# Second attention of a two-layer encoder: score products with packed rows, and a set of four 32-row rotary products between two units' full ones

## The chip, the cores and the metric

One NeuronCore of a Trainium2 chip runs the whole program in one launch. The time is the device time of one execution in microseconds; the smaller the better. Matrix products run on PE (TensorE), whose weight loads the profile calls PEld; DVE is VectorE, ACT is ScalarE, POOL is GpSimd, and SP is the queue that issues most DMAs.

## The reference

Two layers over x of shape (1, 1024, 1024) in float32. Layer A is a dilated window attention; layer B, which the change touches, is a latent attention with 16 heads:

```python
def mixer_mla(u, w_in, q_norm, w_uq, kv_norm, w_ukv, w_out):
    cq, ckv, k_rope, gate = jnp.split(u @ w_in, [256, 256 + 128, 256 + 128 + 32], axis=-1)
    q = (rmsnorm(cq, q_norm) @ w_uq).reshape(B, S, 16, 64 + 32)
    q_nope, q_rope = q[..., :64], q[..., 64:]
    kv = (rmsnorm(ckv, kv_norm) @ w_ukv).reshape(B, S, 16, 64 + 64)
    k_nope, v = kv[..., :64], kv[..., 64:]
    q_rope = rope(q_rope, cos[:, None], sin[:, None])
    k_rope = rope(k_rope, cos, sin)              # one rotary key for all heads
    # per block of 128 queries, per head
    s = (q_nope . k_nope + q_rope . k_rope) * 96 ** -0.5
    o = softmax(s) @ v
    return (o * silu(gate)) @ w_out
```

(The two sums of products are written here with a dot.) Each layer ends with `x <- LayerNorm(alpha * x + gate_c * mixer(u))`.

## The kernel before

Every float32 product is made of three products in PE's faster float32 form: an operand is split into a high part (the rounded value) and a low part (the rest), and high x high, high x low and low x high are added in PSUM (`mm3`; its three lines L92 to L94 appear under those numbers in the profile wherever it is called).

The program runs layer A's attention, its gate and output, then layer B's latents (`layer_b_in`), its gate (`gate`), the second attention (`layer_b_attention`) and the output (`layer_b_out`). The order of PE and SP is the order in which the code is written (`FIXED`); on ACT, DVE and POOL a scheduler chooses the order when the program is built. `weave` interleaves generators of PE work by the costs that they yield.

The second attention works in 128 units of one head (`u // 8`) and one block of 128 queries (`u % 8`). Two heads are a pair of heads `p`; two units, below, a pair of units. For a unit:

- `front(u)`: scores of 128 queries by 1024 keys into an `s` tile of two PSUM banks (two such tiles): for each half of the keys `mm3` with 128 rows, of which 64 hold the head's own part and 64 the rotary part of two heads (32 of the 64 rows of the key are zeros for the wrong head);
- `soft(u)`: DVE takes the row maximum `mb`; `expo(u)`: ACT makes the exponential `pr` and its sum `den`;
- `middle(u)`: PE transposes `pr` in eight 128x128 pieces into two banks `t` (four banks serve `t`, `o` and the projections `m`); ACT casts the high part `pth`, DVE subtracts for the low part `ptl`;
- `back(w)`: for a pair of units, sixteen products of 256 columns with V into `o`; ACT copies out two pieces `osum`, POOL adds them and multiplies the gate `gT`. `spread` sends the reciprocal sums through DRAM to `rden`, with which POOL multiplies later (`normalise`).

Between units run the projections for the next heads: `b_turn` (rotary rows of q for four heads: PE, four DVE products with cos and sin, POOL sums), `b_qk` (q and k of two heads) and `b_v`. For each head the key tiles `kb` (three in turn) got the shared rotary key rows by a POOL copy, `b_rope_rows`. `kb`, `pr`, `osum`, `ab`, `rope` come from a pool `H` of 14 tiles; `q`, `pth`, `ptl`, `vq`, `gT`, the latents `lat` from a pool `G` of 33.

Of the kernel before, what the change touches and what calls it, by code (L numbers as in the profile page):

```python
# [23 lines left out]
P = 128  # L24
# [45 lines left out]
class Trunk:  # L70
# [944 lines left out]
    def layer_b_in(self):  # L1015
# [11 lines left out]
        self.kb = [[self.ht(F32R, "kb") for _ in range(2)] for _ in range(2)]  # L1027

# [22 lines left out]
        nc.gpsimd.memset(latn, 0.0)  # L1051
        ln = [latn[:, 0:512], latn[:, 512:1024]]

        def latents(i):
# [8 lines left out]
            tmp = self.M.tile([P, 64], F32, tag="krt", bufs=2, name=self.nm("krt"))  # L1063
# [19 lines left out]
        def latents_t(i):  # L1083
# [5 lines left out]
            for e, (h, l) in enumerate(self.kb):  # L1089
                dst.append((h[64:128, c : c + P], l[64:128, c : c + P], slice(64 - 64 * e, 128 - 64 * e), 3))  # L1090
            for h, l, rows, j in dst:
                src = pt[rows, j * P : j * P + P]
                nc.scalar.copy(h, src)
                nc.vector.tensor_tensor(l, src, f32(h), op=ALU.subtract)

# [18 lines left out]
        self.wu, self.wv, self.q, self.gT = {}, {}, {}, []  # L1114
# [16 lines left out]
        for b in range(8):  # L1131
# [14 lines left out]
            if b == 0:  # L1146
                self.kb.append([self.ht(F32R, "kb") for _ in range(2)])
                self.b_rope_rows(2)
# [10 lines left out]
        weave((chain(gate(6, 1, self.mbank), gate(7, 1, self.mbank)), 10368.0), (chain(self.b_turn(0), self.b_qk(0)), 9000.0))  # L1159
# [78 lines left out]
    def b_turn(self, p):  # L1238


        nc = self.nc
        r1 = self.ht(F32, "rope")
        self.rope = {p: [], p + 1: [r1[64:128, 0:512], r1[64:128, 512:1024]]}
        for hf in range(2):
# [10 lines left out]
            r0 = ab[64:128, 512:1024]  # L1255
            for dst, row, op in (
                (r1[64:96, sl], 32, ALU.subtract),
                (r1[96:128, sl], 96, ALU.add),
                (r0[32:64], 64, ALU.add),
                (r0[0:32], 0, ALU.subtract),  # L1260
            ):
                nc.gpsimd.tensor_tensor(dst, ab[row : row + 32, 0:512], ab[row : row + 32, 512:1024], op=op)
            self.rope[p].append(r0)

    def b_qk(self, p):

# [4 lines left out]
        qe = [self.gt(F32R, "q") for _ in range(2)]  # L1271
        qo = [self.gt(F32R, "q") for _ in range(2)]
        self.q[2 * p], self.q[2 * p + 1] = qe, qo
        ke, ko = self.kb[(2 * p) % 3], self.kb[(2 * p + 1) % 3]
        rr = self.rope.pop(p)

        def put(dst, sl, src):
            nc.scalar.copy(dst[0][0:64, sl], src)
            nc.vector.tensor_tensor(dst[1][0:64, sl], src, f32(dst[0][0:64, sl]), op=ALU.subtract)

        def rope(hf, part):
            sl = slice(hf * 512, hf * 512 + 512)
            for q in (qe, qo):
                if part == 0:
                    nc.scalar.activation(q[0][64:128, sl], rr[hf], AF.Copy)
                else:
                    nc.gpsimd.tensor_tensor(q[1][64:128, sl], rr[hf], f32(q[0][64:128, sl]), op=ALU.subtract)

        if p:
            self.b_rope_rows(2 * p)  # L1290
            self.b_rope_rows(2 * p + 1)
# [24 lines left out]
    def layer_b_attention(self):  # L1316
# [4 lines left out]
        def front(u):  # L1321
# [7 lines left out]
            if t == 7:  # L1329
                self.q.pop(hd)  # L1330
# [349 lines left out]
```

## Time and profile before

| | |
|---|---|
| time, median of 3 runs | 1356.77 us (1356.26 to 1359.17) |
| profiled execution | 1356.85 us, its span 1355.1 us |
| PE busy | 1328.6 us, 98% of the span |
| PEld, DVE, ACT, POOL busy | 1143.5, 855.9, 799.1, 565.3 us |
| granted clock of PE | 0.994 mean |
| second attention, first to last score product | 776.2 to 1244.7 us |

A row of a timeline has the start in the span, the duration, engine, source line, operation, out<-in, sizes and count; in brackets the time that the engine was idle before it and what ended that. A product's row shows how long it is in the array and its pipeline, not what the next one waits.

### The profile page before, as it was taken

The page shows a single profiled execution, that of the slowest core. Times are in us where ns is not written, and L with a number is a line of the kernel's source. Part 1 is how long each engine was busy: PE and PEld are TensorE (multiplying, and loading weights), DVE is VectorE, ACT ScalarE, POOL GpSimd, SP SyncE. Part 2 cuts the span into 40 slices and gives each one's busy share as a digit, 9 for nine tenths or more (in the row PEclk, how much of TensorE's full clock was granted, in tenths as well). Part 3 has the DMA queues.
Part 4 walks back from the last instruction along what each step waited for, and adds up shares of the span by engine and source line. Part 5 has one row for each costly group of instructions (what it writes and reads, how often), then busy time and mean ns, then how long its engine had stood idle before and what let it go on. Part 6 is the DMA issues. An engine that isn't in the chain of part 4 may idle for free.

```text
span 1355.1 us, 20458 instructions
## 1 busy us (share of the span) xinstructions
PE 1328.6 (98%) x7435; PEld 1143.5 (84%) x7435; DVE 855.9 (63%) x1480; ACT 799.1 (59%) x1631; POOL 565.3 (42%) x552
## 2 busy tenths in 40 slices
PE   9999999999999999999999999999999999999997
PEld 7888888888888888888988888898889889898776
DVE  7645445445544345376733378878787788777887
ACT  4665556544444423165632397889698878887411
POOL 0333123213231477425533444734654473444861
PEclk8999999999999999999999999999999999999999
DMA  9423211113244374371163011111121111113322
GB/s 369 146 35 64 33 58 54 49 27 126 96 132 132 92 179 160 124 252 47 50 182 115 2 33 34 24 38 25 32 52 28 30 25 28 25 55 124 110 93 93
DMA packets 45117, 114.30 MB, mean 84 GB/s; under 512 B 6893, under 2 KB 13342, under 8 KB 45017
## 3 DMA queue, kind: packets, MB, share of 16 engines
q1 hardware_dynamic: 40204, 100.41, 24.0%
q0 software_dynamic: 4192, 12.27, 3.7%
q8 instruction: 59, 0.97, 0.3%
q14 instruction: 42, 0.34, 0.1%
q10 hardware_dynamic: 620, 0.31, 0.1%
HBM read 96.43 MB, written 8.67 MB: 78 GB/s over the span
## 4 chain that ended last, share of the span: by engine, by line
PE 78%; DVE 7%; ACT 7%; DMA 3%; issue 3%; SPq 0%; ACTq 0%; DVEq 0%
PE pj L92 8%; PE pj L94 8%; PE pj L93 8%; PE o L1396 6%; PE t L1376 5%; PE po L92 4%; PE po L93 4%; PE po L94 4%; PE s L92 3%; PE s L94 3%; PE s L93 3%; PE pg L92 2%; PE pg L93 2%; PE pg L94 2%; PE ip L272 2%
## 5 line engine op out<-in xcount | busy, mean ns | idle before, releaser
L92 PE MATMUL pj<-uh,wh 128*128 128x512 f32 x528 | 217.2, 411 | 0.7 <-ACT wh L104 0.7
L94 PE MATMUL pj<-uh,wl 128*128 128x512 f32 x528 | 207.0, 392 | 0.0
L93 PE MATMUL pj<-ul,wh 128*128 128x512 f32 x528 | 206.8, 392 | 0.0
L1336 DVE TENSOR_REDUCE mb<-s 128x1 f32<-128x1024 f32 x128 | 155.8, 1217 | 48.7 <-PE s L94 47.9
L1380 DVE TENSOR_TENSOR ptl<-t,pth 128x512 fp32r<-128x512 f32 x256 | 165.3, 681 | 5.2 <-ACT pth L1379 3.0
L1379 ACT CAST pth<-t 128x512 fp32r<-128x512 f32 x256 | 139.5, 590 | 37.4 <-PE t L1376 34.0
L1344 ACT ACTIVATE pr<-s,mb 128x1024 f32<-128x1024 f32 x128 | 144.2, 1126 | 15.4 <-DVE mb L1336 14.7
L105 POOL TENSOR_TENSOR wl<-wraw,wh 128x1024 fp32r<-128x1024 f32 x42 | 106.3, 2536 | 102.4 <-ACT wh L104 75.4
L1376 PEld LDWEIGHTS t<-ident,pr 128*128 128x128 f32 x1024 | 119.3, 141 | 19.1 <-DVE ptl L1380 2.8
L1376 PE MATMUL t<-ident,pr 128*128 128x128 f32 x1024 | 133.1, 273 | 2.1 <-DVE ptl L1380 2.1
L1396 PE MATMUL o<-pth,vq 128*128 128x256 f32 x512 | 130.4, 292 | 1.1 <-DVE ptl L1380 1.1
L1396 PE MATMUL o<-ptl,vq 128*128 128x256 f32 x512 | 125.6, 283 | 0.8 <-DVE ptl L1380 0.5
L564 ACT ACTIVATE sb<-sb,stat 128x256 f32<-128x256 f32 (+1 forms) x144 | 67.0, 466 | 94.8 <-DVE stat L558 94.7
L94 PEld LDWEIGHTS pj<-uh,wl 128*128 128x128 f32 x528 | 99.1, 188 | 22.2
L1407 POOL TENSOR_TENSOR osum<-osum 64x256 f32<-64x256 f32 x64 | 47.9, 748 | 163.7 <-ACT osum L1406 162.6
L92 PEld LDWEIGHTS pj<-uh,wh 128*128 128x128 f32 x528 | 99.7, 189 | 15.1 <-ACT wh L104 1.1
L93 PEld LDWEIGHTS pj<-ul,wh 128*128 128x128 f32 x528 | 99.8, 189 | 14.0
L92 PE MATMUL s<-kb,q 128*128 128x512 f32 x256 | 105.8, 413 | 0.1
L94 PE MATMUL s<-kb,q 128*128 128x512 f32 x256 | 100.4, 392 | 0.0
L93 PE MATMUL s<-kb,q 128*128 128x512 f32 x256 | 100.4, 392 | 0.0
L1396 PEld LDWEIGHTS o<-ptl,vq 128*128 128x128 f32 x512 | 97.8, 191 | 1.7 <-DVE ptl L1380 1.7
L1396 PEld LDWEIGHTS o<-pth,vq 128*128 128x128 f32 x512 | 97.6, 191 | 1.8 <-DVE ptl L1380 1.7
(289 smaller groups left out, 3128.2 us busy)
## 6 DMA issues: line engine op xcount, KB each, us to landing
wraw<-wa SPq DMA_DIRECT2D x36, 512.0 KB
ada<-ada_row SPq DMA_DIRECT2D x64, 256.0 KB
wraw<-wo_a SPq DMA_DIRECT2D x18, 512.0 KB
ada<-ada_ss SPq DMA_DIRECT2D x16, 512.0 KB
kb<-kb POOLq DMA_DIRECT2D x30, 256.0 KB, 4.5
f<-f_d SPq DMA_DIRECT2D x18, 256.0 KB
xr<-x SPq DMA_DIRECT2D x8, 512.0 KB
xn_d<-z POOLq DMA_DIRECT2D x8, 512.0 KB, 4.5
```

What stands on the lines that cost most here:

```text
L92: mm(out, wh, xh, start=start, stop=False)
L93: mm(out, wh, xl, start=False, stop=False)
L94: mm(out, wl, xh, start=False, stop=stop)
L105: (lo_engine or self.nc.gpsimd).tensor_tensor(l[:, :width], raw[:, :width], f32(h[:, :width]), op=ALU.subtract)
L564: nc.scalar.activation(sb[:, a * w : a * w + w], sb[:, a * w : a * w + w], AF.Exp, bias=stat[:, 0, hh, t : t + 1], scale=-1.0, accum_out=s ...
L1336: nc.vector.tensor_reduce(m[:, 0:1], s, axis=AX.X, op=ALU.max, negate=True)
L1344: nc.scalar.activation(pr, s, AF.Exp, bias=m[:, 0:1], accum_out=dens[u // 8][:, u % 8 : u % 8 + 1])
L1376: nc.tensor.transpose(pt[:, c * P : c * P + P], pr[:, kt * P : kt * P + P], self.ident)
L1379: nc.scalar.copy(h, src)
L1380: nc.vector.tensor_tensor(l, src, f32(h), op=ALU.subtract)
L1396: nc.tensor.matmul(po[:, 0:256], v, pts[j][x][:, c * 256 : c * 256 + 256], start=n == 0, stop=n == 15)
L1407: nc.gpsimd.tensor_tensor(w3[mine, 0:256], w3[mine, 256:512], w3[mine, 0:256], op=ALU.add)
```

## The change

The score product is laid out anew. For a head there are now two key tiles and two query tiles of 128 rows, and a shared key tile `kr`:

- `k[0]` holds the high part of the head's 64 key rows twice, `qa` the high and the low part of the query: one product gives high x high and low x high;
- `k[1]` holds the low part of the 64 rows, 32 rows of the low part of the rotary key and 32 of its high part, `qb` the query's high part, the rotary query's high part and its low part;
- what is left, rotary high x rotary high, has 32 rows. `kr` holds the high rotary key in four groups of 32 rows (groups 0 and 2 the first 512 keys, 1 and 3 the others), `q3` the rotary query's high part likewise (groups 0 and 1 for the even block, 2 and 3 for the odd). The four products of a pair of units each take one group of rows of the array (`tile_position=(32 * g, 0)`) and one PSUM bank.

`front` now does a pair of units: four full products, the set of four, four full products. The loop steps by pairs, and the second unit's exponential is issued ahead of `back`. The rotary rows of q go through a DRAM tile `rope_d`, from which `qb` and `q3` are loaded; rows that stand twice are copied by a DMA on SP (for the first pair of heads by a second ACT cast). POOL's per-head copies of key rows go. `b_turn(0)` runs in one weave with the gate's next to last product, `b_qk(0)` with the last.

```diff
-            for c in (400, 448):
-                nc.vector.tensor_tensor(t[:, c : c + 16], tmp[:, 0:16], tmp[:, 32:48], op=ALU.subtract)
-                nc.vector.tensor_tensor(t[:, c + 32 : c + 48], tmp[:, 16:32], tmp[:, 48:64], op=ALU.add)
+            rot = t[:, 384:512].rearrange("p (g a c) -> p g a c", g=4, a=2)
...
+            for rows in ((slice(0, P),) if i < 4 else (slice(32, 64), slice(96, 128))):
+                nc.scalar.copy(self.kr[rows, sl], pt[rows, 3 * P : 4 * P])
...
-        weave((chain(gate(6, 1, self.mbank), gate(7, 1, self.mbank)), 10368.0), (chain(self.b_turn(0), self.b_qk(0)), 9000.0))
+        weave((gate(6, 1, self.mbank), 5184.0), (self.b_turn(0), 2600.0))
+        weave((gate(7, 1, self.mbank), 5184.0), (self.b_qk(0), 3900.0))
...
-    def b_rope_rows(self, hd):
-        for src, dst in zip(self.kb[(hd - 2) % 3], self.kb[hd % 3]):
-            self.nc.gpsimd.dma_start(dst[64:128, :], src[64:128, :])
+    def b_rope_rows(self):
+        dma, first = self.nc.gpsimd.dma_start, self.kb[0][1]
+        for j in range(2):
+            dma(first[96:128, j * 512 : j * 512 + 512], self.kr[32 * j : 32 * j + 32, :])
+        for n in (1, 2):
+            dma(self.kb[n][1][64:128, :], first[64:128, :])
...
+            engine = nc.gpsimd if p else nc.vector
+            for rows, op in ((slice(0, 64), ALU.subtract), (slice(64, 128), ALU.add)):
+                engine.tensor_tensor(ab[rows, 0:512], ab[rows, 0:512], ab[rows, 512:1024], op=op)
+            yield 0.0
+            hl = self.ht(F32R, "rope")
+            nc.scalar.activation(hl[:, 0:512], ab[:, 0:512], AF.Copy)
+            engine.tensor_tensor(hl[:, 512:1024], ab[:, 0:512], f32(hl[:, 0:512]), op=ALU.subtract)
+            for a in range(2):
+                for x in range(2):
+                    nc.sync.dma_start(rd[:, x, a, :, sl], f32(hl[64 * a : 64 * a + 64, x * 512 : x * 512 + 512]))
...
+            nc.sync.dma_start(f32(qb[64:128, :]), rows.rearrange("x a c t -> (x a c) t"))
+            q3 = third[:, e * 512 : e * 512 + 512]
+            for g in range(4):
+                src = rows[0].rearrange("a c (i z t) -> (a c) i z t", z=2, t=P)[:, :, g // 2, :]
+                nc.sync.dma_start(f32(q3[32 * g : 32 * g + 32, :]).rearrange("p (i t) -> p i t", t=P), src)
...
+        def both(dst, twin, sl, src, rows):
+            nc.scalar.copy(dst[0:64, sl], src)
+            if p:
+                nc.sync.dma_start(f32(twin[rows, sl]), f32(dst[0:64, sl]))
+            else:
+                nc.scalar.copy(twin[rows, sl], src)
...
+            def full(a):
+                ts = slice((t + a) * P, (t + a) * P + P)
+                for n, (q, kk) in enumerate(((qa, k[0]), (qb, k[1]))):
+                    for j in range(2):
+                        ks = slice(j * 512, j * 512 + 512)
+                        mm(s[a][:, ks], q[:, ts], kk[:, ks], start=n == a == 0, stop=n == a == 1)
+                st[u + a] = s[a]
+            full(0)
+            for g in range(4):
+                rows = slice(32 * g, 32 * g + 32)
+                ks = slice((g % 2) * 512, (g % 2) * 512 + 512)
+                mm(
+                    s[g // 2][:, ks], q3[rows, (t // 2) * P : (t // 2) * P + P], self.kr[rows, :],
+                    start=g >= 2, stop=g < 2, tile_position=(32 * g, 0),
+                )
+            full(1)
...
+        for u0 in range(0, nu + 4, 2):
+            if u0 < nu:
+                front(u0)
...
+                soft(u0)
+                soft(u0 + 1)
+                expo(u0)
+            for u in (u0, u0 + 1):
...
+                if 0 <= u - 2 < nu:
+                    middle(u - 2)
+                    next(vprep, None)
+                if u == u0 and u < nu:
+                    expo(u + 1)
+                if u == u0 and u >= 4:
...
+                    back((u - 4) // 2)
```

On PE, unit 82 before stood like this: six full products of 128 rows into its score tile, then the transposes of an earlier unit's exponential.

```order
L92 MATMUL s_1738_10422<-kb_830_5410,q_1653_10014 128x512
L93 MATMUL s_1738_10422<-kb_831_5411,q_1653_10014 128x512
L94 MATMUL s_1738_10422<-kb_830_5410,q_1654_10015 128x512
L92 MATMUL s_1738_10422<-kb_830_5410,q_1653_10014 128x512
L93 MATMUL s_1738_10422<-kb_831_5411,q_1653_10014 128x512
L94 MATMUL s_1738_10422<-kb_830_5410,q_1654_10015 128x512
L1376 MATMUL t_1744_10435<-ident_71,pr_1725_10363 128x128 x4
L1376 MATMUL t_1745_10442<-ident_71,pr_1725_10363 128x128 x4
```

On PE, units 82 and 83 now (`s_1747` and `s_1748` are their score tiles; L1357 is the 32-row set):

```order
L1350 MATMUL s_1747_10472<-kb_830_5410,q_1665_10069 128x512 x2
L1350 MATMUL s_1747_10472<-kb_831_5411,q_1666_10070 128x512 x2
L1357 MATMUL s_1747_10472<-kr_5412,q3_1664_10068 128x512 x2
L1357 MATMUL s_1748_10473<-kr_5412,q3_1664_10068 128x512 x2
L1350 MATMUL s_1748_10473<-kb_830_5410,q_1665_10069 128x512 x2
L1350 MATMUL s_1748_10473<-kb_831_5411,q_1666_10070 128x512 x2
L1408 MATMUL t_1756_10496<-ident_71,pr_1730_10404 128x128 x4
L1408 MATMUL t_1757_10503<-ident_71,pr_1730_10404 128x128 x4
```

Two units' scores, which were twelve full products in two places, are eight full ones with the set of four between them, in one place.

On ACT, the same units before: the exponentials (`pr`) with the casts of transposed tiles (`pth`) and the copies of `o` (`osum`) between them.

```order
L1344 ACTIVATE pr_1746_10449,den_1724_10362<-s_1738_10422,mb_1739_10429 128x1024
L1357 COPY rden_1748_10469<-o_1747_10451 4x128
L1405 COPY osum_1749_10473<-o_1747_10451 64x256
L1406 COPY osum_1749_10473<-o_1747_10451 64x256
L1379 CAST pth_1740_10431<-t_1755_10500 128x4x128
L1379 CAST pth_1742_10433<-t_1756_10507 128x4x128
L1344 ACTIVATE pr_1757_10514,den_1724_10362<-s_1752_10486,mb_1754_10498 128x1024
```

On ACT, these units now:

```order
L1376 ACTIVATE pr_1751_10490,den_1729_10403<-s_1747_10472,mb_1749_10486 128x1024
L1411 CAST pth_1752_10492<-t_1756_10496 128x4x128
L1376 ACTIVATE pr_1758_10510,den_1729_10403<-s_1748_10473,mb_1750_10488 128x1024
L1411 CAST pth_1754_10494<-t_1757_10503 128x4x128
L1389 COPY rden_1760_10531<-o_1759_10513 4x128
L1437 COPY osum_1761_10535<-o_1759_10513 64x256
L1438 COPY osum_1761_10535<-o_1759_10513 64x256
```

The second exponential moved ahead of the copies of `o`, with one cast between the two exponentials.

On ACT at the start of the attention before (`pg_960` is the gate's last product, `m` the projections that become q and k, `ab` the rotary rows, `s_963` the first score tile):

```order
L1278 CAST q_956_6643<-m_961_6682 64x512
L1285 ACTIVATE q_954_6641<-ab_953_6632 64x512
L1285 ACTIVATE q_956_6643<-ab_953_6632 64x512
L1128 ACTIVATE gT_946_6565<-pg_960_6672 128x512
L1221 CAST vq_964_6735<-m_968_6739 128x4x2x64
L1344 ACT_TABLE_LOAD
L1344 ACTIVATE pr_971_6749,den_970_6748<-s_963_6728,mb_969_6746 128x1024
```

On ACT at the same place now (`pg_955` is the gate's last product, `s_965` the first score tile, `q_957` and `q_958` are `qa` and `qb` of the first head):

```order
L1135 ACTIVATE gT_946_6539<-pg_955_6635 128x512
L1302 CAST q_957_6640<-m_961_6654 64x512
L1306 CAST q_958_6641<-m_961_6654 64x512
L1302 CAST q_957_6640<-m_963_6689 64x512
L1306 CAST q_958_6641<-m_963_6689 64x512
L1302 CAST q_959_6647<-m_961_6654 64x512
L1306 CAST q_960_6648<-m_961_6654 64x512
L1302 CAST q_959_6647<-m_963_6689 64x512
L1306 CAST q_960_6648<-m_963_6689 64x512
L1376 ACT_TABLE_LOAD
L1376 ACTIVATE pr_975_6753,den_974_6752<-s_965_6723,mb_972_6748 128x1024
```

The casts that make q of the first two heads moved from ahead of the gate's last activation to behind it.

More of the change, by code (lines that the diff above doesn't have):

```diff
@@ L1295, in b_qk @@
             yield 1300.0
-            put(qe, sl, ps[0:64, :])
-            put(qo, sl, ps[64:128, :])
+            for e, (qa, qb, k) in enumerate(heads):
+                src = ps[64 * e : 64 * e + 64, :]
+                both(qa, qb, sl, src, slice(0, 64))
+                nc.vector.tensor_tensor(qa[64:128, sl], src, f32(qa[0:64, sl]), op=ALU.subtract)
             yield 0.0
-            rope(hf, 0)
             ps = self.mbank()
```

151 lines of the change are left out of this document (63 added, 88 removed).

## The prediction, as put on record before the run

> **What bounds the kernel now.** I read the page's shares first, then the busy times by stretch, then TensorE's timeline over some pairs of units of the second attention, and last ACT's and DVE's timelines there.
>
> ```profile
> span 1355.1 us, 20458 instructions
> PE 1328.6 (98%) x7435; PEld 1143.5 (84%) x7435; DVE 855.9 (63%) x1480; ACT 799.1 (59%) x1631; POOL 565.3 (42%) x552
> ...
> 1020.00:1060.00 40.00, 39.50 (x265) 35.44 (x264) 30.54 (x42) 34.52 (x71) 17.37 (x20) 1.00 0.10 24
> 1060.00:1100.00 40.00, 39.13 (x262) 34.65 (x261) 33.49 (x47) 29.89 (x60) 23.12 (x24) 1.00 0.13 26
> ```
>
> In a stretch the columns are length, then busy time of PE, PEld, DVE, ACT and POOL, granted clock, DMA share. PE is busy 98% at clock 1.00, so only PE time that is taken out shortens the attention; ACT (34.5 of 40) and DVE (33.5 of 40) come next.
>
> ```profile
> L92 PE MATMUL s<-kb,q x256: 389/395/504, 776.2 to 1244.3; 128*128 128x512 f32 x128
> ...
> 1002.99 0.40 PE L92 MATMUL s<-kb,q 128*128 128x512 f32 x1
> 1003.22 0.40 PE L93 MATMUL s<-kb,q 128*128 128x512 f32 x1
> ...
> 1004.15 0.40 PE L94 MATMUL s<-kb,q 128*128 128x512 f32 x1
> 1004.38 1.03 PE L1376 MATMUL t<-ident,pr 128*128 128x128 f32 x8
> 1005.17 0.47 PE L92 MATMUL s<-kb,q 128*128 128x512 f32 x1
> 1005.49 0.39 PE L93 MATMUL s<-kb,q 128*128 128x512 f32 x1
> ...
> 1006.64 1.04 PE L1376 MATMUL t<-ident,pr 128*128 128x128 f32 x8
> 1007.43 0.36 PE L1396 MATMUL o<-pth,vq 128*128 128x256 f32 x1
> 1007.63 0.28 PE L1396 MATMUL o<-ptl,vq 128*128 128x256 f32 x1
> ...
> 1009.42 0.27 PE L1399 MATMUL o<-ident,den 128*4 128x128 f32 x1
> 1009.45 0.48 PE L92 MATMUL s<-kb,q 128*128 128x512 f32 x1
> ```
>
> The mean duration of a product (0.39 us) is not its price: they overlap, and the next starts 0.23 us later (six from 1002.99 to 4.38: 1.39/6 = 0.2317). Eight transposes take 0.79 us (1004.38 to 5.17), 0.099 each, every one with a weight load of its own. After transposes the first product costs 0.32 instead of 0.23 (1005.17 to 5.49): 0.09 us for a weight load that nothing covers. The sixteen products with V take 1.99. One pair: 12 x 0.2317 + 0.09 + 2 x 0.79 + 1.99 = 6.44 us, and the trace has 1002.99 to 1009.45 = 6.46, with no gap. With the projections between them the 64 pairs take from 776.2 to 1244.7, 7.3 us each.
>
> **The change, part by part.**
>
> *Removed and added on PE.* A pair had 12 full products of scores (3 kinds x 256 = 768 in all) and gets 8, plus four 32-row ones that lie in four row groups of the array and write four banks. That removes 4 x 0.2317 = 0.927 us a pair and adds the set, which no row of this trace shows. Its lower end is one full product, 0.23 (all four run at once). Its upper end is four in a row and an uncovered load on either side, as at a transpose: 0.93 + 2 x 0.09 = 1.11. A gain beyond the lower end is excluded, since 512 columns must still be streamed. Between them I go by the weight loads: each of the four has its own, and the nearest rows, the transposes, take one every 0.099. The product ahead of the set covers two (0.23/0.099), two are left: the last of the four starts 0.198 after the first and streams 0.23, then the return to the full array costs one uncovered load. 0.198 + 0.232 + 0.09 = 0.52. So 0.927 - 0.52 = 0.41 a pair, x 64 = **26 us**.
>
> *Second exponential ahead of the products with V, and both units in one step.* Now PE runs full products, set, full products, 8 transposes, 16 products with V, 8 transposes. Does the set's second half wait for the score bank of the unit before? Rows for the pitches of ACT and DVE:
>
> ```profile
> 1001.70 0.59 ACT L1379 CAST pth<-t 128x512 fp32r<-128x512 f32 x1
> 1002.18 1.12 ACT L1344 ACTIVATE pr<-s,mb 128x1024 f32<-128x1024 f32 x1
> 1003.19 0.20 ACT L1344 ACTIVATION_READ_ACCUMULATOR pr<-s,mb 128x1 f32 x1
> 1003.28 0.59 ACT L1379 CAST pth<-t 128x512 fp32r<-128x512 f32 x1
> 1003.89 0.37 ACT L1405 COPY osum<-o 64x256 f32<-64x256 f32 x1
> ...
> 1011.12 1.23 DVE L1336 TENSOR_REDUCE mb<-s 128x1 f32<-128x1024 f32 x1 [1.79 <-PE s L94]
> 1012.26 1.28 DVE L1380 TENSOR_TENSOR ptl<-t,pth 128x512 fp32r<-128x512 f32 x2
> 1013.46 1.22 DVE L1336 TENSOR_REDUCE mb<-s 128x1 f32<-128x1024 f32 x1
> ```
>
> Start to start: exponential 1.10, cast 0.48, maximum 1.14, two subtractions 1.20. From the pair's start F: first unit's scores at F+1.6, its maximum to 2.8, exponential 2.9 to 4.0, two casts to 5.0, second exponential 5.0 to 6.1. The next pair starts at F+6.0 and needs that bank at its set, F+7.0: 0.9 us to spare. The transposes use four banks in turn; the tightest reuse is that of the pair's last four, which take the bank of its first four: wanted at F+5.6, read by DVE up to F+5.25, 0.35 us to spare. ACT needs 2 x 1.10 + 4 x 0.48 + 2 x 0.37 = 4.9 of 6.0 us a pair, DVE 2 x 1.14 + 2 x 1.20 = 4.7. Hidden, while these margins hold; if they go, the bank is what is late next.
>
> *Preparation of queries and keys.* Before, ACT and POOL wrote the rotary rows of each head:
>
> ```profile
> L1278 ACT CAST q<-m 64x512 fp32r<-64x512 f32 x24 | 14.0, 582 | 4.6 <-DVE q L1279 4.5
> L1285 ACT ACTIVATE q<-ab 64x512 fp32r<-64x512 f32 x12 | 6.9, 620 | 0.1
> L1285 ACT ACTIVATE q<-rope 64x512 fp32r<-64x512 f32 x12 | 6.9, 620 | 0.1
> ...
> 1010.01 0.24 SPq L1358 DMA_DIRECT2D den_d<-rden  x1
> 1011.27 0.45 SPq L1359 DMA_DIRECT2D rden<-den_d  x1
> ```
>
> Of these, four ACT casts per pair of heads (4 x 0.62) go, and one 128x512 cast per half and two pairs of heads comes; POOL's subtractions and its copies of key rows go. SP gets 18 transfers per pair of heads and 8 more per two of them: 22 x 0.24 to 0.45 = 5 to 10 us of issuing in eight pairs (54 us). A write and the read that waits for it lie 1.26 us apart (1010.01 to 1011.27). The heads' rows are ready over one pair, some 7 us, ahead of use, so these hops are hidden. What queues behind a waiting SP transfer are the denominators' two; their reader is POOL, half idle, and PE waits for neither. Priced at nothing. In the three stretches with a rotation on POOL, the exponentials stand behind a cast that waits for it: I add 1 us in all.
>
> *The start of the attention* is not hidden:
>
> ```profile
> 774.53 0.58 ACT L1278 CAST q<-m 64x512 fp32r<-64x512 f32 x1
> 776.58 1.15 ACT L1285 ACTIVATE q<-ab 64x512 fp32r<-64x512 f32 x2 [1.46 <-POOL ab L1262]
> 777.75 0.60 ACT L1128 ACTIVATE gT<-pg 128x512 f32<-128x512 f32 x1
> ...
> 775.99 0.69 DVE L1279 TENSOR_TENSOR q<-m,q 64x512 fp32r<-64x512 f32 x1
> ...
> 776.02 0.39 PE L94 MATMUL pg<-u1h,wgl 128*128 128x512 f32 x1
> 776.24 0.39 PE L92 MATMUL s<-kb,q 128*128 128x512 f32 x1
> 779.12 1.28 ACT L1344 ACT_TABLE_LOAD   x1
> ```
>
> Before, the casts of q stood ahead of the last gate's activation; now all eight stand behind it (the order of ACT, above). The gate's last product ends at 776.41; then activation 0.60, cast 0.58, DVE's subtraction 0.69: the first score product at 778.3 instead of 776.24, 2.1 us. Seven casts (3.4) and the table load (1.28) then hold the first exponential, so that the second and third pair's sets wait some 0.6 us each: 3.3 us, less the 0.5 us (39.5 of 40) that PE already loses there: **+3 us**. The rest (latents, output projection) keeps its PE rows under a busy PE: nothing.
>
> **Sum.** -26 + 3 + 1 = -22. The profiled execution took 1356.85 (span 1355.1), 0.1 above the median 1356.77. I predict 1356.8 - 22 = **1334 us**.
>
> **Against the Trainium skill.** After transposes the trace's return to full products costs 0.09 us, and I charge the same once for the set. The Trainium skill, "TensorEngine Tiling (Array Packing)", section Tiling Modes, states that a change of the tiling mode drains TensorE; no run here shows it yet. It is the third rival below. The same skill's "TensorE: Matmul & The Clock Gate", Part 3, gives 3.07x for four 32-row products of 512 columns; an estimate by it is 0.93/3.07 = 0.30 for the set and, with 0.09, about 1322 us. That speaks for the first rival.
>
> **Rivals.**
> 1. *All four at once.* The loads of the set run ahead of all four: 0.232 + 0.09 = 0.32, 0.61 a pair, -39 + 4: **1322 us**. For it: weight loads do run under products in this trace (PEld 84% beside PE 98%). Against: nowhere here are more than one known to be ahead. Chance 0.25.
> 2. *Slower: the row groups run one after another.* Set 0.93, loads 0.18: 1.11 against 0.927 removed, +0.18 x 64 = +12, +4 of the start: **1373 us**. It decides from a set of 0.86 us on (0.927 - 4/64). For it: every product in this trace starts only after the one ahead has streamed. Against: none here lies in a row group of its own. Chance 0.15.
> 3. *A drain on both sides of the set.* A product's row ends 0.39 after its start, 0.16 after the next one's; paid twice, instead of the 0.09: 0.43 + 0.32 = 0.75, 0.18 a pair, -11 + 4: **1350 us**. Chance 0.13.
> 4. *The banks of the transposes.* If the 0.35 us of margin goes and each pair loses 0.3, the gain shrinks by 19: **1353 us**. For it: ACT and DVE at 84 to 86% of the stretch, and their stretch gets 6% shorter. Chance 0.07.
>
> **Numbers.** The forecast's own case (set between 0.4 and 0.65, 1326 to 1342) has 0.40. A measurement here tells about 0.2%, 2.7 us, from no change. Faster: 0.40 + 0.25 + 0.13 + most of 0.07 = 0.82; slower 0.15; the same 0.03. The range runs from a set at its lower end with no uncovered load (0.695 x 64 = 44, less 4: 1317) to rival 4 with some spread: **1316 to 1356**, which leaves the slower rival out.
>
> **What would show it.** After: 512 full score products and 256 of 32 rows; the step from the set's first start to the next full product reads 0.32 (rival 1), 0.5 (forecast), 0.75 (3) or 1.1 (2). A pair without projections takes 6.05 us. PE idles 2 us ahead of the first score product, behind DVE's q. Wrong would be: PE waiting within each pair for DVE's ptl (rival 4) or PE's share falling under 95%.

## The result and the profile after

The changed kernel takes 1377.05 us (median of 4 runs, 1376.94 to 1377.24), the kernel before 1357.97 beside it: **19 us slower**, ratio 1.0138 (95% interval 1.0119 to 1.0158). The forecast was 1334. The page of the profiled execution, then the groups of the score products, and the stretches that the prediction quoted for the kernel before (columns: length, busy time of PE, PEld, DVE, ACT, POOL, granted clock, DMA share):

```profile
span 1375.2 us, 20612 instructions
PE 1321.1 (96%) x7435; PEld 1104.8 (80%) x7435; DVE 871.9 (63%) x1462; ACT 788.0 (57%) x1611; POOL 489.1 (36%) x479
```

```profile
L1350 PE MATMUL s<-kb,q x512: 387/396/796, 785.1 to 1261.1; 128*128 128x512 f32 x171
L1357 PE MATMUL s<-kr,q x256: 489/491/792, 790.7 to 1259.8; 32*128 32x512 f32 x128
```

```profile
1020.00:1060.00 40.00, 37.90 (x273) 32.19 (x272) 31.12 (x42) 32.04 (x65) 11.93 (x14) 1.00 0.10 29
1060.00:1100.00 40.00, 37.99 (x252) 30.77 (x251) 31.00 (x42) 32.87 (x65) 14.23 (x16) 1.00 0.27 68
```

PE did become 7.5 us less busy, but it now stands idle 2.1 us in each 40 (0.5 and 0.9 before), and the attention begins at 785 in place of 776. ACT and DVE are about as busy as before.

To place the loss I cut both executions at the first product of the latents and at the exponentials of pairs of units 0, 4 and 60. These rows are from the timelines of PE and ACT, first of the kernel before, then of the changed one:

```profile
637.10 0.43 PE L92 MATMUL plat<-wlh,u1h 128*128 128x416 f32 x1
780.42 1.12 ACT L1344 ACTIVATE pr<-s,mb 128x1024 f32<-128x1024 f32 x1
802.69 1.12 ACT L1344 ACTIVATE pr<-s,mb 128x1024 f32<-128x1024 f32 x1
1221.28 1.13 ACT L1344 ACTIVATE pr<-s,mb 128x1024 f32<-128x1024 f32 x1
```

```profile
640.70 0.43 PE L92 MATMUL plat<-wlh,u1h 128*128 128x416 f32 x1
792.83 1.12 ACT L1376 ACTIVATE pr<-s,mb 128x1024 f32<-128x1024 f32 x1 [4.21 <-DVE mb L1368]
817.07 1.12 ACT L1376 ACTIVATE pr<-s,mb 128x1024 f32<-128x1024 f32 x1 [0.45 <-DVE mb L1368]
1240.68 1.11 ACT L1376 ACTIVATE pr<-s,mb 128x1024 f32<-128x1024 f32 x1
```

| stretch, us | before | after | difference | forecast | step of two alone |
|---|---|---|---|---|---|
| up to the first product of the latents | 637.1 | 640.7 | +3.6 | 0 | 637.5 |
| from there to the first exponential | 143.3 | 152.1 | **+8.8** | +2 | 143.8 |
| pair 0 to pair 4 | 22.3 | 24.2 | +1.9 | 0 | 24.2 |
| pair 4 to pair 60 | 418.6 | 423.6 | **+5.0** | -22 (-23 + 1 for the rotations) | 433.4 |
| from there to the end of the span | 133.8 | 134.5 | +0.7 | -2 | 135.0 |

(The last column is the experiment order_alone, below.) The 3.6 us of the first row lie in code that the change does not touch, and profiles of kernels with that code unchanged stand between 636.1 and 641.8. I count them as spread, though the changed kernel's own four runs lie within 0.3 us of each other, so they may belong to this build. So two things failed: the start, and above all the pairs.

**The pairs.** A pair without projections, on PE:

```profile
1218.74 1.17 PE L1350 MATMUL s<-kb,q 128*128 128x512 f32 x4
1219.83 0.50 PE L1357 MATMUL s<-kr,q 32*128 32x512 f32 x4
1220.26 1.19 PE L1350 MATMUL s<-kb,q 128*128 128x512 f32 x4
1221.29 1.03 PE L1408 MATMUL t<-ident,pr 128*128 128x128 f32 x8
...
1224.98 1.17 PE L1350 MATMUL s<-kb,q 128*128 128x512 f32 x4
```

The set runs 0.43 us (1219.83 to 1220.26), and the twelve products of a pair 2.55 (1218.74 to 1221.29) where the twelve full ones took 2.86 (1.39 behind the products with V and 1.47 behind transposes): 0.31 us gained, 0.41 forecast. The whole pair gains 0.2: it takes 6.24 to 6.33 us instead of 6.44 to 6.54, mainly since in every other one the products with V start some 0.17 us late, behind DVE's `ptl`. So where nothing else runs, the change is a gain, of half the size forecast.

The four products of a set start together: each takes 0.49 us (the group L1357 above), all four 0.50. The weight loads on either side of the set start late, while four loads of full products follow each other without a gap (0.76 us):

```profile
1218.71 0.76 PEld L1350 LDWEIGHTS s<-kb,q 128*128 128x128 f32 x4
1219.83 0.19 PEld L1357 LDWEIGHTS s<-kr,q 32*128 32x128 f32 x4 [0.36 <-issue]
1220.26 0.76 PEld L1350 LDWEIGHTS s<-kb,q 128*128 128x128 f32 x4 [0.24 <-issue]
```

PEld stands idle 0.36 us ahead of the set's loads and 0.24 ahead of those of the next full products, each time until the product itself starts.

With projections in a pair the change does not gain. Eight pairs (one pair of heads) of the kernel before, without and with a rotation in them, then the same of the changed one:

```profile
894.20:953.90 59.70, 59.21 (x400) 53.26 (x399) 46.76 (x66) 51.56 (x103) 26.80 (x31) 1.00 0.15 36
833.40:894.20 60.80, 59.57 (x388) 52.63 (x387) 49.83 (x69) 48.81 (x98) 34.91 (x37) 1.00 0.13 29
```

```profile
910.30:971.50 61.20, 58.08 (x401) 48.47 (x400) 47.63 (x65) 49.32 (x99) 19.15 (x23) 1.00 0.20 52
848.80:910.30 61.50, 58.28 (x389) 47.94 (x388) 50.21 (x69) 47.68 (x95) 25.50 (x28) 1.00 0.24 64
```

Length less PE's busy time: PE stood idle 0.5 and 1.2 us before, 3.1 and 3.2 us after. The added idle time (2.6 and 2.0) is more than what its busy time fell by (1.1 and 1.3). The chart of waits names for whom it waits, in pairs 4 to 60, in the kernel before and after:

```profile
PE m L92 <- DVE kb L1306: 3.3, 7, 0.5
PE t L1376 <- DVE ptl L1380: 2.1, 3, 0.8
```

```profile
PE t L1408 <- DVE ptl L1412: 7.3, 7, 1.1
PE o L1428 <- DVE kb L1325: 6.2, 7, 0.9
PE t L1408 <- ACT osum L1438: 3.8, 6, 0.9
PE o L1428 <- DVE ptl L1412: 1.5, 3, 0.5
```

Transposes and products with V wait for DVE's subtractions of the transposes (`ptl`) and of a k projection (`kb`), and for ACT's `osum`: the four banks that `t`, `o` and the projections share come free too late. One such place of the changed kernel, on DVE and then on PE:

```profile
948.19 1.38 DVE L1325 TENSOR_TENSOR kb<-m,kb 64x512 fp32r<-64x512 f32 x2
...
949.72 0.36 PE L1428 MATMUL o<-pth,vq 128*128 128x256 f32 x1 [0.88 <-DVE kb L1325]
```

DVE's next `ptl` starts at 951.47, behind a subtraction for q and a maximum.

**The start.** PE's first score products, the chain of waits ahead of them, and SP's queue:

```profile
785.07 1.22 PE L1350 MATMUL s<-kb,q 128*128 128x512 f32 x2 [4.35 <-DVE q L1315]
789.59 1.19 PE L1350 MATMUL s<-kb,q 128*128 128x512 f32 x2 [3.30 <-DMA q<-rope_d]
790.71 1.01 PE L1357 MATMUL s<-kr,q 32*128 32x512 f32 x4
```

```profile
777.63 8.11 DMA rope_d<-rope
785.94 3.51 DMA q<-rope_d
```

```profile
769.98 8.25 SPq L1275 DMA_DIRECT2D rope_d<-rope  x8
```

The last of the eight transfers of the rotated rows, 128 KB each, lands in DRAM 8.1 us after it is issued (777.63), and the rows take 3.5 back. The second pair of products waits 3.30 us for them, after the first pair has waited 4.35 for DVE's q. Behind these gaps PE's clock is down:

```profile
785.00:789.00 4.00, 1.22 (x2) 0.50 (x2) 1.39 (x3) 3.58 (x6) 0.00 (x0) 0.50 0.37 97
789.00:795.00 6.00, 5.41 (x24) 4.02 (x25) 3.22 (x4) 1.90 (x4) 0.00 (x0) 0.65 0.64 169
795.00:800.00 5.00, 5.00 (x36) 4.08 (x36) 4.05 (x6) 3.15 (x7) 0.74 (x1) 1.00 0.07 25
```

The granted clock reads 0.50, then 0.65, and 1.00 in the stretch from 795 on; the first set takes 0.94 us (790.71 to 791.65) instead of 0.43. That agrees with the Trainium skill, "TensorE: Matmul & The Clock Gate", section HAM oscillation, by which idle gaps of more than some 3.4 us bring the clock to half; the first gap here is 4.35, and the second, 3.30, comes while the clock is down.

### The profile page after: what moved, and what is told of

Same layout as the page of the kernel before. It is cut to its first block, busy times and chain, and to the rows that moved or that the text cites. A ratio compares the mean times of both kernels' runs of the same rounds, so it can differ in the third digit from the quotient of the medians.

```text
span 1375.2 us, 20612 instructions
## 1 busy us (share of the span) xinstructions
PE 1321.1 (96%) x7435; PEld 1104.8 (80%) x7435; DVE 871.9 (63%) x1462; ACT 788.0 (57%) x1611; POOL 489.1 (36%) x479
## 4 chain that ended last, share of the span: by engine, by line
PE 72%; DVE 13%; ACT 5%; DMA 5%; issue 4%; SPq 1%; POOL 0%; ACTq 0%; DVEq 0%; POOLq 0%
PE pj L92 8%; PE pj L94 8%; PE pj L93 8%; PE o L1428 5%; PE s L1350 5%; PE t L1408 4%; DVE mb L1368 4%; PE po L92 4%; PE po L93 4%; PE po L94 4%; DVE ptl L1412 3%; PE ip L272 2%; DMA ada<-ada_row 2%; PE t L575 2%; PE pg L92 2%
## 5 line engine op out<-in xcount | busy, mean ns | idle before, releaser
L1368 DVE TENSOR_REDUCE mb<-s 128x1 f32<-128x1024 f32 x128 | 155.2, 1219 | 18.4 <-PE s L1357 17.4
L1350 PE MATMUL s<-kb,q 128*128 128x512 f32 x512 | 151.6, 418 | 7.9 <-DVE q L1315 4.3
L1408 PE MATMUL t<-ident,pr 128*128 128x128 f32 x1024 | 135.9, 274 | 11.3 <-DVE ptl L1412 7.3
L1350 PEld LDWEIGHTS s<-kb,q 128*128 128x128 f32 x512 | 88.3, 190 | 36.9 <-issue 19.6
L104 ACT ACTIVATE wh<-wraw 128x1024 fp32r<-128x1024 f32 x54 | 57.1, 1058 | 50.4 <-DMA wraw<-wa 29.0
```

The lines of the kernel that those rows point to most:

```text
L1350: mm(s[a][:, ks], q[:, ts], kk[:, ks], start=n == a == 0, stop=n == a == 1)
L1368: nc.vector.tensor_reduce(m[:, 0:1], s, axis=AX.X, op=ALU.max, negate=True)
L1408: nc.tensor.transpose(pt[:, c * P : c * P + P], pr[:, kt * P : kt * P + P], self.ident)
```

## The experiments

Each theory's expectation is quoted as written ahead of its run. The kernel before measured 1356.4 to 1358.6 us beside them.

### First four: start, set, early exponential, step of two

*early_turn*: the rotation for the first heads beside the gate's block 5.

```diff
+ if b == 5:
+     weave((gate(5, 1, self.mbank), 5184.0), (self.b_turn(0), 2600.0))
...
- weave((gate(6, 1, self.mbank), 5184.0), (self.b_turn(0), 2600.0))
- weave((gate(7, 1, self.mbank), 5184.0), (self.b_qk(0), 3900.0))
+ weave((chain(gate(6, 1, self.mbank), gate(7, 1, self.mbank)), 10368.0), (self.b_qk(0), 5000.0))
```

> The changed kernel, with the first rotation of queries (b_turn(0)) woven with the gate's block 5 instead of block 6, so that its way through DRAM lies some 16 us earlier; everything from the second pair of units on is the same. Theory A (the start is the largest loss: first score product 8.8 us later than before, and 5.7 us more to the fourth pair, since the casts of q and the loads from DRAM end late): the first score product comes at 776 to 778 us and the time falls by 11 to 14 us, to 1363 to 1366. Rival B (the start's wait is only the visible end of a slower pace; ACT and DVE, behind anyway, set the time): the first score product comes earlier, but the time falls by less than 4 us.

*no_set*: the four 32-row products (high times high of the rotary term) left out.

> The changed kernel without the four 32-row products (the rotary high x high part of the scores is left out); queries, keys, transfers and order are the same. Theory A (PE sets the pace outside a few waits; the set costs 0.61 us a pair in an undisturbed pair, 0.43 for itself and 0.18 in the products on either side): 64 x 0.61 = 39 us less, near 1338, and an undisturbed pair at 5.7 us. Rival B (DVE and ACT set the pace, 6.2 us a pair): less than 15 us, 1362 or more, the pairs stay near 6.1.

*exp_behind*: `expo(u0 + 1)` behind `back`.

> The changed kernel with the second unit's exponential written behind the products with V, as the other half of the order was before. Theory A (the early exponential is what frees the second score bank in time for the set): the set waits for it in most pairs, 0.2 to 0.5 us each, 10 to 30 us slower, 1387 to 1407. Rival B (the early exponential holds up ACT's casts of transposed tiles, and so the transposes' banks): faster by 3 to 10 us. If the scheduler hides either: within 3 us.

*order_alone*: the kernel before's products and layout, in the changed kernel's loop over two units (`front(u0)`, `front(u0 + 1)`, and the second exponential ahead of `back`).

> The kernel before (twelve full score products a pair, POOL's copies of key rows, no transfers through DRAM, the start as before) with only the loop of the changed one: both units' scores together, second exponential ahead of the products with V, projections at the same points. Theory A (the waits of PE for DVE and ACT in the pairs with projections, about 3 us in each eight pairs, come from the stepping by pairs): slower by 12 to 25 us, 1370 to 1382, with the waits 'o <- kb' and 't <- ptl' of about 1 us in the same pairs. Rival B (they come from the packed layout, its copies and transfers): within 4 us of the kernel before.

Measured: early_turn 1372.28 us (1.0085 to 1.0119 of before), no_set 1359.76 (1.0004 to 1.0026), exp_behind 1390.45 (1.0229 to 1.0265), order_alone 1376.03 (1.0124 to 1.0154).

- early_turn takes 4.8 us off, less than theory A asked for and more than rival B. Its first exponential stands at 786.2 in place of 792.8 (the first product of the latents at 640.7 in both), with no idle time ahead of the scores: of the start's 8.8 us, 6.6 were the DRAM hop and the late casts of q, which this run moves together.
- order_alone settles the largest term. Without any packing the step of two costs 18 us. Its pairs without projections take 6.42 and 6.52, as before, so the step costs nothing there; eight pairs take 62.1 and 62.9 because of waits in the projections' pairs, the same two that the changed kernel has:

```profile
PE t L1376 <- DVE ptl L1380: 7.6, 10, 1.7
PE o L1396 <- DVE kb L1306: 6.5, 7, 1.2
```

  Against this kernel the packing does gain: 433.4 to 423.6 between pairs 4 and 60, 9.8 us.
- no_set is the check on what a PE that is faster still would bring. It takes 256 products away and gains 17 us, not the 39 of theory A, nor the less than 15 of rival B:

```profile
903.10:961.20 58.10, 53.92 (x368) 47.65 (x367) 47.33 (x65) 49.05 (x98) 19.14 (x23) 1.00 0.22 54
```

  PE is 4.2 us less busy in eight pairs than in the changed kernel and idle 4.2 instead of 3.1; even without the set it does not beat the kernel before.
- exp_behind: with the second exponential behind the products with V, 13 us more, as theory A said. In the changed kernel the early one is needed.

### Do the row groups run side by side?

*one_group*: all four in the first row group.

```diff
- s[g // 2][:, ks], q3[rows, ...], self.kr[rows, :], ..., tile_position=(32 * g, 0),
+ s[g // 2][:, ks], q3[0:32, ...], self.kr[0:32, :], ..., tile_position=(0, 0),
```

> The changed kernel with all four 32-row products of a set in the first row group of the array (they read the first 32 rows of both tiles, so part of the rotary term is replaced by another; the work is the same). If the row groups overlap, as the 0.43 us from the set's first product to the next full one says: here the four run one after another, 0.93 us and more, +0.5 a pair, and the time rises by 15 to 32 us to 1392 to 1409. If they don't (the second rival): 1375 to 1379 as before.

1397.66 us (1.0277 to 1.0315), 20.6 more than the changed kernel. On PE:

```profile
1207.06 1.19 PE L1357 MATMUL s<-kr,q 32*128 32x512 f32 x4
1208.18 1.19 PE L1350 MATMUL s<-kb,q 128*128 128x512 f32 x4
```

The same four take 1.12 us in one group and 0.43 in four. They overlap: the second rival is false, though its time, 1373, lies nearest to the result. The 0.69 us more are 44 us in 64 pairs, but the time rose by 20.6 only, since PE's idle time between pairs 4 and 60 fell from 20.1 to 5.4 us: the longer set stands where PE waited before.

### The place of the projections

*spread*: both q products at the end of one pair, their copies in the next, then one k product a pair. *spread_early* adds the early turn, *order_spread* does it to order_alone. *one_a_pair*: one product a pair behind the scores.

```diff
+ half = [slice(0, 512), slice(512, 1024)]
+ pq = [self.b_product(w, 0, sl) for sl in half]
+ yield 2600.0
...
- if r == 8:
-     prep = self.b_qk(p + 1)
+ if r == 7:
+     qprep = self.b_qk(p + 1)
```

> The changed kernel with the projections of q and k laid out otherwise in the attention: both q products stand at the end of the pair of units r = 6, their copies after the next pair's first transposes, then one k product at the end of each of the next two pairs with its copies in the pair after. No work is left out. Theory A (stepping two units at once puts a projection's products and copies so close together that TensorE waits for their copies, about 19 us of TensorE waits in the six blocks and some per block more in the longer pairs): most of that goes, eight pairs take 59 to 59.8 instead of 61.5, and the time is 1358 to 1366 (11 to 19 less than the changed kernel's 1377). Theory B (ACT and DVE have too much to do in those pairs, wherever the products stand): 1373 to 1379.

> The same with the rotation for the first heads moved beside the gate's block 5 and the first q and k products beside blocks 6 and 7, as in the run with the early turn. Theory A: the start and the projection pairs cost independently, so 4 to 8 us less than the run with the projections spread alone: 1351 to 1360. Theory B: what one place gives the other takes, within 2 us of the spread run.

> The kernel before's products and layout in steps of two units (1376.0 as run), with the projections of q and k laid out as in the spread run. Theory A: the 18 us that the step of two units costs come from the projections' place, so 1358 to 1364 here. Theory B: they come from the step itself (scores of two units in a row, both score banks wanted at once): 1372 to 1378.

> The changed kernel with one projection product per pair of units, right behind the scores, its copies behind the next two transposes, from r = 6 to r = 12, and no second bank of a projection ever held. No work is left out. Theory A: fewer banks are held at a time, so 1360 to 1368. If the copies that the scheduler leaves far apart on ACT (the two casts of one q product stand five to nine instructions apart) hold the one bank as long as before: 1370 to 1380.

All four missed: 1400.09 (median of three runs), 1392.92, 1417.04 and 1400.98 us. By the code, two projections' banks held at a time leave the transposes with two (the blocks have pairs of up to 13 us), and with one product a pair the q and k work runs into the rotation's; neither reason was tested. The place matters, but my rule for it was wrong.

### Banks or copies?

*free_bank*: the same copies, read from SBUF, so that a projection's bank is free at once.

```diff
- src = ps[64 * e : 64 * e + 64, :]
+ src = (fake if p else ps)[64 * e : 64 * e + 64, :]   # fake: a latents tile in SBUF
```

> The changed kernel in which, from the second pair of heads on, the copies and subtractions of the q and k projections read a tile of the latents in SBUF in place of the projections' PSUM banks (so those heads' scores are of other numbers): the same products, the same number of instructions on ACT and DVE, in their order as scheduled, but a projection's bank comes free at once. Theory A (the four banks shared by transposes, o and projections are what TensorE waits for): the waits for kb and ptl in the q and k pairs go, 12 to 18 us less than the changed kernel's 1377: 1359 to 1365. Theory B (ACT's and DVE's work itself delays the maxima, exponentials and casts): within 5 us, 1372 to 1378.

*staged*: one cast and one subtraction of 128 rows per projection into a staging tile, DMAs onward; *one_staged* the same on one_a_pair.

```diff
- two casts and two subtractions of 64 rows, each from ps
+ x = self.ht(F32R, "qst")
+ nc.scalar.copy(x[:, 0:512], ps)
+ nc.vector.tensor_tensor(x[:, 512:1024], ps, f32(x[:, 0:512]), op=ALU.subtract)
+ ... six nc.sync.dma_start of 64 rows
```

> The changed kernel in which, from the second pair of heads on, each projection bank is read by one cast and one subtraction of all 128 rows into a staging tile, and DMAs carry the rows to the q and k tiles: two instructions in place of four on ACT and DVE, and the bank is free after them. No work is left out. Theory A (banks) and theory B (load of ACT and DVE) both say faster here, A by 10 to 16 us (1361 to 1367), B by 5 to 9 (the 4.6 us of casts and 5.5 us of subtractions per pair of heads are half its drain): 1368 to 1372. If the longer SP queue (24 transfers of some 0.4 us more per pair of heads) delays the rows: 1377 or more.

> One product per pair of units and the staging tile together. Theory A: the projections then cost little beyond their products, 1353 to 1360, eight pairs in 59 us. If it is no better than the better of the two by itself, the rest of the loss is not in the q and k projections.

free_bank: 1378.33, no gain, as theory B said. The waits for `kb` go and those for `ptl` grow in their place:

```profile
PE t L1409 <- DVE ptl L1413: 16.7, 19, 1.9
```

So it does not help to free the projections' own banks. That points to their copies on ACT and DVE, which delay the copies of the transposes, whose banks are late then; it does not show it, since the scheduler also moved the copies, which no longer depend on a product. staged: 1373.75 (1.0094 to 1.0150), 3 us less than the changed kernel with overlapping intervals, in neither theory's range; its blocks without a rotation take 58.9 us instead of 61.2, those with one 61.1 to 63.6. one_staged: 1390.64, 10 less than one_a_pair. Less copying helps, in blocks without a rotation.

### The order on ACT and DVE

*written* and *order_written*: ACT and DVE in the order of the code, on the changed kernel and on order_alone.

```diff
- with tc.manual_schedule(engines=FIXED):
+ with tc.manual_schedule(engines=FIXED | {mybir.EngineType.Activation, mybir.EngineType.DVE}):
      self.layer_b_attention()
```

> The changed kernel with ACT's and DVE's instructions of the second attention in the order in which the code is written, in place of the order that the scheduler made at build time (and one more empty step in the rotation, so that its cast on ACT stands behind POOL's sums). The same instructions, all of the work. Theory S (TensorE's waits in the pairs with projections come from where the scheduler put the projections' copies among the maxima, exponentials and transposes' copies): eight pairs take 59 to 60.3 in place of 61.2, 1363 to 1371 in all, against the changed kernel's 1377. Theory L (the amount of ACT's and DVE's work per pair is the limit, in any order): 1375 or more.

> The kernel before's products and layout in steps of two units (1376.0 as run with the scheduler's order), with ACT's and DVE's instructions in the written order. Theory S: a good part of the 18 us that the step costs goes, 1360 to 1369. Theory L, or a limit in the score banks: 1374 to 1380.

1455.53 and 1458.79 us: 78 and 83 slower with the same instructions. The written order was a bad one, but it shows how much the order alone moves. *hand_early* then put the copies where the margins of the trace ask for them (`osum` behind the next casts `pth`, the copies of q right behind their product), with the early turn; *hand3* kept the scheduler's order in the first 8 and the last 16 units:

> The changed kernel with the early rotation, and the written order mended by hand: the copies of the products with V stand behind those of the next transposes in pairs without a projection, the copies of a q product directly behind it, the casts of a k product ahead of the next maxima and its subtractions behind them, the rotation's four products with cos and sin in two portions. All of the work. Theory S: eight pairs take 58 to 59.5, and with the 8 us of the early start 1348 to 1359, faster than the changed kernel by 18 or more. Theory L: 1366 to 1373, as the early rotation by itself (1372).

> The run hand_early with two edits: the order by hand only in units 8 to 111, and the two casts of a q product directly after each other. Theory S: it takes back the 9 us that hand_early lost ahead of unit 8 and behind unit 111, and little in the blocks (60 and 63 for eight pairs): 1367 to 1372.

hand_early 1380.03 (in neither theory's range), hand3 1372.65 (1.0099 to 1.0130; early_turn has 1372.28). Pairs without projections fall to 6.14 and 6.24 us, but eight pairs take 60.1 and 63.1. Order by hand does no better than the scheduler in total.

*hand2* (with staging, the later rotations spread over four pairs and the rotated rows read back last) and *hand4* (hand3 with the staging tile alone):

> The run hand_early with four more edits, all of the work kept: the order by hand only in units 8 to 111, the scheduler's order ahead of them and behind; each projection's bank read by one cast and one subtraction of 128 rows (as in the staged run); the later rotations begun four units earlier, their bank copied out at once by ACT and their products with cos and sin spread over four pairs; the rotated rows of q read back at the end of the projections. Theory S (order and place of the copies are what TensorE waits for, and the amount of work is not): eight pairs take 58.0 to 59.5 and the time is 1345 to 1358, at or under the kernel before. Theory L: eight pairs 60 or more, 1364 or more.

> The run hand3 with one edit: from the second pair of heads on, each projection's bank is read by one cast and one subtraction of 128 rows into a staging tile, and DMAs carry the rows on (24 more transfers per pair of heads on SP's queue). All of the work. If the projections' copies on ACT and DVE are what delays the transposes' copies, and with them TensorE, then half of their work at the same places takes most of TensorE's waits of 3 us per eight pairs: eight pairs without a rotation 58.3 to 59, with one 61 to 62, and 1358 to 1364 in all. If only the order counts, or the transfers are late instead: 1369 to 1376.

hand2: 1378.02; PE waited 10.8 us in three places for the rows that I had moved to the end of SP's queue. hand4: 1377.97 us (1.0140 to 1.0170), in neither range in all, but its blocks tell the two theories apart. Without a rotation, then with one:

```profile
905.20:963.60 58.40, 57.47 (x405) 48.79 (x403) 44.43 (x61) 45.30 (x94) 17.88 (x22) 1.00 0.36 90
838.20:905.20 67.00, 60.30 (x384) 48.70 (x383) 47.66 (x65) 44.91 (x92) 26.56 (x29) 0.95 0.36 90
```

Without a rotation eight pairs take 58.4 (all three such blocks: 58.4 to 58.5), as expected, and the waits of PE for `ptl` and `kb` are gone: what is left there is 1.0 us for `vq` and `osum`. The changed kernel takes 61.2 there, with half the copies alone 58.9 (staged), with the order by hand alone 60.1 (hand3): in those blocks the amount of the copies is the larger part of the loss. (The staging also frees a projection's bank after two reads in place of four.) With a rotation the staging tile itself is late, because SP's queue still carries the rotated rows:

```profile
985.76 9.79 SPq L1287 DMA_DIRECT2D rope_d<-rope  x7
...
1002.80 2.53 SPq L1308 DMA_DIRECT2D q<-rope_d  x4
...
1008.65 0.58 SPq L1332 DMA_DIRECT2D q<-qst  x1
```

```profile
1014.44 0.59 ACT L1344 CAST qst<-m 128x512 fp32r<-128x512 f32 x1 [4.96 <-DMA q<-qst]
```

ACT stands 4.96 us behind a transfer, with the exponentials behind it. No version here beat the kernel before; the best packed ones are early_turn and hand3.

## Why the prediction was wrong, point by point

- **The set** (0.52 a pair, bounds 0.23 to 1.11): the size was near, the reason was not. Eight full products at 0.2317 and 0.09 behind transposes leave 2.55 - 1.85 - 0.09 = 0.61 for it. The gain is 0.31 a pair, 6 us less over pairs 4 to 60 than forecast. That "the last of the four starts 0.198 after the first" failed: the four start within 0.01 us of each other, as the first rival had it. That the step from the set's first start to the next full product reads 0.43, near the forecast's 0.5, is luck. The first rival's price (0.32) and the forecast's both have an uncovered load on one side of the set only; the trace has late loads on both. The third rival, a drain on both sides, asked for a step of 0.75, which is too much, but a weaker form of it shows in the ends that the profile gives: the set starts 0.08 us ahead of the end of the full product before it (1219.83 against 1219.51 + 0.40), and the next full one 0.07 ahead of the set's end (1220.26 against 1219.83 + 0.50), where full products overlap by 0.16. By the Trainium skill's 3.07x ("TensorE: Matmul & The Clock Gate", Part 3) the set would take an estimated 0.30 of four products in a row of 0.93; here it is 0.43 against 1.12 measured in one group, 2.6x. (By the forecast's own sum that 0.30 gives 1326 us, not the 1322 written there.)
- **"Second exponential ahead of the products with V, and both units in one step ... Hidden, while these margins hold"**: this step failed, and with it the sign. I worked the margins (0.9 and 0.35 us) out for a pair without projections, where they held but for the 0.17 us in every other one, and did not work out the 24 of 64 pairs that hold projections, nor those behind them that still hold their copies. order_alone puts the step's price there at 14.8 us between pairs 4 and 60, and 1.9 ahead of them, with none of it in the pairs that I had looked at.
- **"Preparation of queries and keys ... Priced at nothing"**: failed in the same place. I compared ACT's and DVE's totals with the pair's length. These totals are about what they were: between pairs 4 and 60 DVE has 338 us for 334, ACT 339 for 352. What counts is the place: the projections' copies stand ahead of `ptl` on DVE, as between 948 and 951 us above. Of the packing's 0.31 x 56 = 17.4 us, 9.8 are left against order_alone.
- The sum from pair 4 to 60: -23 forecast (56 x 0.41), + 5.6 for the set's size, + 14.8 for the step of two, and a remainder of 7.6 make the measured +5. Of the remainder 1.9 shows as idle time of PE (18.3 us in order_alone, 20.1 here). The rest lies within PE's rows, in short waits such as the 0.17 us, and was not broken down further.
- **The start** (+3): PE did wait behind DVE's q, 4.35 us for the 2.1 forecast, since four casts of the last k product (ACT, 780.37 to 782.73) stand ahead of the gate's last activation; the forecast's chain left them out. For the second wait, of 3.30, the step that failed is "A write and the read that waits for it lie 1.26 us apart": that row was of a few denominators; here the last write, of 128 KB, landed 8.1 us after its issue and the read took 3.5. For the first heads these are not hidden. With the clock after the gaps, the start lost 8.8 us, of which early_turn took back 6.6. The 1.9 us more by pair 4 belong to the step of two: order_alone has the same 24.2.
- **The fourth rival**, the banks of the transposes, named the right wait and had 0.07. I priced it as a smaller gain (1353), since I allowed it 0.3 us a pair evenly; it came in the projections' pairs, and cost more than the packing gave. "PE waiting within each pair for DVE's ptl" was given as the sign of a wrong forecast; it showed in the pairs with projections. PE's share fell to 96%, not under 95.
- What stays open: why the step of one unit tolerates the same copies. That a unit's scores stand there between a projection's product and the next use of its bank fits order_alone, but was not tried by itself. Nor was it tried which half of the step costs, the scores of two units in a row or the moved exponential, without the packing. In the blocks with a rotation the cause was not separated further: in the block shown PE waits 6.2 us for `ptl` in hand4 and 2.8 in hand3.

## What to carry to other kernels

A margin that is worked out for the plain step of a loop says nothing of the steps that carry extra work; when two units are joined into one step, lay out the step with the most copies, queue by queue, since there a bank comes free late although no engine is full. Try a reordering by itself before a saving is put on top of it: here it cost 18 us without the packing and hid what the packing gave. And price a trip through DRAM by a transfer of its own size, not by a small one from another place.

## What the runs showed of the hardware

- Four 32-row products of 512 columns in four row groups, among full ones: they start within 0.01 us of each other, and the next full product 0.43 us later; with both edges the set costs 0.61. In one row group the step is 1.12 us: starts at 1207.06, 1207.39, 1207.63 and 1207.86, then the next full product at 1208.18, so the inner steps are near a full product's 0.23 and the two at the edges longer.
- Transfers on one queue, issued back to back, take 0.54 to 0.60 us of the queue each for 64 rows by 512 columns; twelve of them took from 1008.65 to 1016.27 in hand4, 7.6 us, and ACT waited 4.96 us behind one.
- The same instructions in another order on ACT and DVE: 1377.05 to 1455.53 us.
